# One encoder layer on TensorE: the weight tiles of the up-projection start 64 (or 112) bytes further on, and the down-projection's activations are loaded straight into their own tiles

## The chip, the cores and the metric

The kernel runs on one core of one Trainium2 chip. The metric is the time of one execution on the device in microseconds: 2622.09 us, the median of 3 runs (2621.0 to 2622.91).

## What is computed

One layer of a transformer trunk over 512 tokens of width 2048, all in float32: an input projection that feeds two attention branches and their gates, an output projection, and then a gated convolutional feed-forward part, which is the part that the change touches.

```python
h2 = rmsnorm(x, norm_ffn[l])
u = h2 @ w_up[l]                       # 2048 -> 2 * 5632
up = jnp.pad(u, ((0, 0), (1, 1), (0, 0)))
u = up[:, :-2] * cw[0] + up[:, 1:-1] * cw[1] + up[:, 2:] * cw[2] + conv_b[l]
gate, val = jnp.split(u, 2, axis=-1)
x = x + (jax.nn.silu(gate) * val) @ w_down[l]   # 5632 -> 2048
```

## The kernel before

**Number format.** Every float32 matrix product is made of three TensorE products of float32r numbers. A tensor is split into `hi`, its rounding to float32r, and `lo`, the rest (`split`, L222 to L233, for activations; `Plain.prep`, L146 to L160, for weights). ScalarE (ACT) makes `hi` with a copy, VectorE (DVE) makes `lo` with a subtraction. The products are hi by hi, hi by lo and lo by hi. All matmuls of the big products are issued by the helper `mm`, so they all stand under line L77 in the profile, and all loads on the queue of SyncE (SP) stand under L74, the helper `dma`, which keeps them in program order.

**Up.** `up(s)` for s from 0 to 21 makes one block of 256 gate and 256 value columns. Its product runs in `products`: 8 units, one for each pair of 128-row slices of the 2048 inputs. A unit has 7 forms of its weights (a scheme with seven products in place of eight), in two groups of 4 and 3. For each form and each half of the columns there are three matmuls, 42 in a unit and 7392 in all 22 blocks. In each of them the weights `wh` or `wl` (128 by 128) are the stationary operand, loaded by a LDWEIGHTS of its own, and 256 columns of a form of the activations, held in a slot `s`, stream past. `Product.load` brings a unit's weights into a tile `f` (4 buffers), and `Product.prep` (L581 to L595) splits them into the tiles `wh` and `wl`. In the built program the 56 slots, `wh` and `wl` all start at multiples of 512 bytes in a partition; the constants FILL and EDGE at the top of the kernel are pads that see to that.

After a block, `combine` copies the seven accumulators out of their PSUM banks (ACT L669, L671, L672 and DVE L666, L677), and the queue of small work does the rest: scaling by the row factor (DVE L828), the convolution (`conv`: six ACT instructions, L836, L838, L839, and then two accumulating DMAs on GpSimd's (POOL's) queue, L840 and L841), SiLU (ACT L853), the product of gate and value (DVE L857) and the store to the DRAM tensor `act[s]` (POOL L858).

**Down.** The 22 pairs of `act` are the activations of the down-projection, in two parts of 11. `down(part, n)` makes 512 output rows with 22 slices of the inner dimension, two in a unit of 24 matmuls; its matmuls stream 512 columns. Before a part runs, `split_act` loads each pair of `act` from DRAM and splits it: for part 0 in the last up block (one pair ahead of each unit from unit 1 on) and in the first four units of down, for part 1 in `down(0, 3)`. The load goes into a buffer `quad("a")`, 128 by 2 by 512, and ACT L227 and DVE L228 split it into four slots. There are two buffers of the tag "a", and they are the same ones into which `conv` writes its two shifted products `before` and `after`; they become free again when the accumulating DMAs L840 and L841 have read them.

Each engine runs its instructions in the order of the built program. On SP a load that waits for a buffer holds up all later loads; on ACT a split that waits for its load holds up all later ACT work.

Of the kernel before, what the change touches and what calls it, by code (L numbers as in the profile page):

```python
# [11 lines left out]
F32 = mybir.dt.float32  # L12
F32R = mybir.dt.float32r
AF = mybir.ActivationFunctionType
ALU = mybir.AluOpType
# [3 lines left out]
P = 128  # L19
# [19 lines left out]
def trunk_kernel(  # L39
# [6 lines left out]
    nc = tc.nc  # L46
# [17 lines left out]
    def slot(dt=F32):  # L64
        return big.tile([P, S], dt, tag="s", name="s", bufs=N_SLOTS)
# [4 lines left out]
    def bank(tag):  # L70
        return banks[tag].tile([P, S], F32, tag=tag, name=tag)

    def dma(dst, src):
        tc.keep_in_program_order(nc.sync.dma_start(dst, src))  # L74

    def mm(o, l, r, start, stop):
        nc.tensor.matmul(o, l, r, start=start, stop=stop, skip_group_check=True)  # L77
# [18 lines left out]
    part = {}  # L96
    for held, names in ((smalls, KEPT), (masks, SMALLS)):
        at = 0
# [16 lines left out]
    steps, units, queue = [], [], deque()  # L115
    at = {"load": 0, "sums": 0, "prep": 0, "use": 0}
# [10 lines left out]
    class Plain:  # L127


        def __init__(self, w, k, kpb, cols):  # L130
            self.w, self.k, self.kpb, self.cols = w, k, kpb, cols
# [14 lines left out]
        def prep(self, *between, pieces=1):  # L146
            self.load(pieces)
            for work in between:
                work()
            hi = wst["p"].tile([P, 1024], F32R, tag="hi", name="hi", bufs=2)  # L150
            lo = wst["p"].tile([P, 1024], F32R, tag="lo", name="lo", bufs=2)
            n = 1024 // pieces
            for c in range(0, 1024, n):
                nc.scalar.copy(hi[:, c:c + n], self.raw[:, c:c + n])  # L154
                nc.vector.tensor_tensor(  # L155
                    lo[:, c:c + n], self.raw[:, c:c + n], hi[:, c:c + n].bitcast(F32),
                    ALU.subtract)
            self.hi = hi.rearrange("p (a n) -> p a n", a=self.kpb)
            self.lo = lo.rearrange("p (a n) -> p a n", a=self.kpb)
# [12 lines left out]
    def advance(*between):  # L172


        prep_to(at["use"] + 1, between)
        for phase, d in (("sums", 2), ("load", 4)):
            while at[phase] < len(products_) and products_[at[phase]].ready(phase, at["use"] + d):
                getattr(products_[at[phase]], phase)()
                at[phase] += 1
        make_early()  # L180

    def next_unit():
        u = units[at["use"]]
        at["use"] += 1
        return u
# [38 lines left out]
    def split(src, alloc=slot, g=None):  # L224
        hi, lo = alloc(F32R), alloc(F32R)
        if g is None:
            nc.scalar.copy(hi, src)  # L227
            nc.vector.tensor_tensor(lo, src, hi.bitcast(F32), ALU.subtract)  # L228
        else:
            last["act"] = nc.scalar.activation(hi, src, AF.Copy, scale=g).ins  # L230
            last["dve"] = nc.vector.scalar_tensor_tensor(
                lo, src, g, hi.bitcast(F32), op0=ALU.mult, op1=ALU.subtract).ins
        return hi, lo  # L233
# [133 lines left out]
    def v_b(pair):  # L367
        raws, res = [], [None] * 2

        def evac(m, ps):  # L370
            v = att.tile([P, S], F32, tag="v", name="v", bufs=4)
            nc.scalar.copy(
                v.rearrange("p (j r c) -> p j r c", j=4, r=8),
                ps.rearrange("p (r j c) -> p j r c", j=4, r=8))
            raws.append(v)

        def head(h):
            v = raws[h].rearrange("p (j r c) -> p j r c", j=4, r=8)
            nc.vector.tensor_tensor(
                v, v, rows["m"].rearrange("p (r j c) -> p j r c", j=4, r=8), ALU.mult)  # L380
            b = bank("tr")
            for j in range(4):
                nc.tensor.transpose(
                    b[:, j * P:(j + 1) * P], raws[h][:, j * P:(j + 1) * P], ident)
            res[h] = split(b)

        step("f", w_in, [(C_VB + pair * 256, 256)], hT, evac,
             post=lambda: queue.extend(partial(head, h) for h in range(2)),
             rate=ATTENTION_RATE)
        return res  # L390
# [143 lines left out]
    v = v_b(0)  # L534
    q_a(1, ka, va)
    for pair in range(4):
        kq_b(pair, v)
        if pair < 3:
            v = v_b(pair + 1)
# [4 lines left out]
    ffn, products_, early, made = {}, [], deque(), deque()  # L544
    keep = tc.keep_in_program_order

    class Product:
# [1 line left out]

        def __init__(self, w, first, kept):
            self.w, self.first = w, first
            self.kept = dram.tile([P, 4, 256], F32, name=f"sums{first}") if kept else None
            self.made = False

# [25 lines left out]
        def prep(self, *between):  # L582
            self.parts = []
            for b, (tag, n) in enumerate((("a", 4), ("b", 3))):
                if between:
                    between[b]()
                hi = ffn["w"].tile([P, n, 256], F32R, tag="h" + tag, name="wh", bufs=2)
                lo = ffn["w"].tile([P, n, 256], F32R, tag="l" + tag, name="wl", bufs=2)
                f = self.f[:, 4 * b:4 * b + n]
                keep(nc.scalar.copy(hi, f))  # L590
                keep(nc.vector.tensor_tensor(lo, f, hi.bitcast(F32), ALU.subtract))  # L591
                self.parts += [(hi[:, i], lo[:, i]) for i in range(n)]
            for work in between[2:]:
                work()
# [16 lines left out]
    def quad(tag):  # L611
        return ffn["q"].tile([P, 2, S], F32, tag=tag, name=tag, bufs=2)
# [18 lines left out]
    def products(w, c, acts, evac, before=None, kept=()):  # L631

        def run():
            ps = []
            for i in range(8):
                if before:
                    before(i)
                u = next_unit()
                for f, (wh, wl) in enumerate(u.parts):
                    if i == 0:  # L640
                        ps.append(bank("mm"))
                    a = acts[i][f]
                    for m in range(2):
                        o, s = ps[f][:, m * 256:(m + 1) * 256], slice(m * P, (m + 1) * P)
                        mm(o, wh[:, s], a[:, :256], i == m == 0, False)
                        mm(o, wh[:, s], a[:, 256:], False, False)
                        mm(o, wl[:, s], a[:, :256], False, i == 7 and m == 1)
                advance(*(combine(ps, evac) if i == 7 else ()))
                run_queued(1)

        steps.append(run)
        v = w.rearrange("(d b p) (h n) -> d p b h n", b=2, p=P, h=2)
        for i in range(8):
            u = Product(v[i, :, :, :, c:c + 256], len(units), i in kept)
            units.append(u)
            products_.append(u)
            if i in kept:
                early.append(u)

    def combine(ps, evac):  # L660

        q1, q2, q4, q5, q7, q6, q3 = [p.rearrange("p (m n) -> p m n", m=2) for p in ps]
        v = lambda: scratch().rearrange("p (m n) -> p m n", m=2)
        top, low, p1, v2 = quad("u"), quad("u"), v(), v()
        left, right = slice(0, 256), slice(256, 512)
        add = lambda *args: keep(nc.vector.tensor_tensor(*args))  # L666

        def one():
            keep(nc.scalar.copy(p1, q1))  # L669
            add(top[:, :, left], q2, p1, ALU.add)  # L670
            keep(nc.scalar.copy(low[:, :, left], q4))  # L671
            keep(nc.scalar.copy(low[:, :, right], q5))  # L672

        def two():
            add(v2, p1, q6, ALU.subtract)
            add(p1, v2, low[:, :, right], ALU.add)
            keep(nc.vector.scalar_tensor_tensor(  # L677
                v2, q7, -1.0, v2, op0=ALU.mult, op1=ALU.subtract))
            add(top[:, :, right], q3, p1, ALU.add)

        def three():
            both = low.rearrange("p m (t n) -> p m t n", t=2)
            add(both, v2.unsqueeze(2).to_broadcast([P, 2, 2, 256]), both, ALU.subtract)
            evac(top, low)

        return one, two, three
# [24 lines left out]
    half = {}  # L711
# [113 lines left out]
    act = [dram.tile([P, 2, S], F32, name=f"act{j}") for j in range(pairs_ff)]  # L825
# [18 lines left out]
    parts = [range(pairs_ff // 2), range(pairs_ff // 2, pairs_ff)]  # L844
    acts = [[], []]
# [33 lines left out]

    def split_act(part, n):  # L880

        if n < len(parts[part]):
            a = quad("a")
            dma(a, act[parts[part][n]])
            acts[part] += [split(a[:, i]) for i in range(2)]

    def down(part, n):
        held = []
# [98 lines left out]
```

## Time and profile before

| | |
|---|---|
| median of 3 runs | 2622.09 us |
| the profiled execution | 2616.16 us |
| its span, first to last instruction | 2614.4 us |
| share of the span that TensorE is busy (PE) | 98% |
| mean granted TensorE clock | 0.993 |
| up, from its first to its last matmul | 1198.6 to 2111.4 us |
| down, from there to the last matmul | 2111.5 to 2610.4 us |

The busy share of PE is high everywhere and says little, because matmuls overlap: a matmul of 256 columns is shown 283 ns long, while the next one starts 120 ns after it. What counts is the distance between starts and the idle time between matmuls. In the groups, the tile names stand as output<-inputs, the streamed operand first: `mm<-s,wh` is a matmul of up, `mm<-s,hi` one of the other products. In the timeline, a row's two first numbers are its start and its length, xN merges N equal instructions, and the bracket gives the engine's idle time before it and what ended that.

### The profile page before, as it was taken

To read this page: it belongs to the slowest core of one execution; us is meant where nothing else is said; L and a number is where in the kernel's file an instruction comes from. 1 tells how busy PE (TensorE), PEld (TensorE's weight loads), DVE (VectorE), ACT (ScalarE), POOL (GpSimd) and SP (SyncE) were. 2 spreads that over 40 slices of the span, in tenths; PEclk is the share of its full clock that TensorE was granted. 3 is DMA by queue.
4 is the path that set the end of the run, shared out by engine and by line. 5 is a ranking of instruction groups with operands and counts; after the bars stand their busy time and mean duration, and the time that the engine had idled before them with its cause. 6 is when DMAs were issued, how large, how long until landed. Compare 5 with 4: busy or idle time off the path is not lost.

```text
span 2614.4 us, 38157 instructions
## 1 busy us (share of the span) xinstructions
PE 2568.2 (98%) x15016; PEld 2287.3 (87%) x15016; DVE 1521.3 (58%) x2155; ACT 1125.1 (43%) x1617; POOL 206.4 (8%) x248
## 2 busy tenths in 40 slices
PE   9999999999999999999999999999999879999999
PEld 7888888888888888888999999999999868888887
DVE  6565554635455567656778778787787543243222
ACT  5355544532222232334555665656656442132111
POOL 0100000000000000100111111111111100000000
PEclk9999999999999999999999999999999989999999
DMA  5322223338777888854677777777777755464443
GB/s 182 97 89 85 90 91 96 91 97 273 246 258 248 260 271 275 293 179 137 172 186 205 194 206 196 193 207 196 203 195 196 213 162 167 145 210 137 129 129 112
DMA packets 291509, 464.66 MB, mean 178 GB/s; under 512 B 22784, under 2 KB 190336, under 8 KB 291328
## 3 DMA queue, kind: packets, MB, share of 16 engines
q1 hardware_dynamic: 246240, 348.00, 42.4%
q0 software_dynamic: 40480, 105.83, 16.4%
q10 hardware_dynamic: 4608, 8.39, 0.8%
q8 instruction: 117, 1.92, 0.3%
q14 instruction: 64, 0.52, 0.1%
HBM read 347.93 MB, written 68.16 MB: 159 GB/s over the span
## 4 chain that ended last, share of the span: by engine, by line
PE 44%; DMA 3%; ACT 2%; issue 1%; DVE 0%; SPq 0%; ACTq 0%; POOLq 0%; DVEq 0%
PE mm L77 44%; DMA o<-a 2%; ACT wh L590 1%; ACT o L836 0%; DMA a<-act 0%; ACT a L838 0%; ACT a L839 0%; DMA f<-sums 0%; DMA raw<-in_w_down 0%; DMA f<-in_w_up 0%; DVE wl L591 0%; ACT t L669 0%; SPq L74 0%; ACT s L227 0%; ACT hi L154 0%
## 5 line engine op out<-in xcount | busy, mean ns | idle before, releaser
L77 PE MATMUL mm<-s,hi 128*128 128x512 f32 x3712 | 1111.1, 391 | 17.8 <-ACT t L669 8.4
L77 PE MATMUL mm<-s,wh 128*128 128x256 f32 x4928 | 848.2, 284 | 18.4 <-ACT wh L590 12.0
L77 PEld LDWEIGHTS mm<-s,hi 128*128 128x128 f32 x3712 | 699.2, 189 | 163.7 <-ACT t L669 8.9
L77 PEld LDWEIGHTS mm<-s,wh 128*128 128x128 f32 x4928 | 730.8, 193 | 20.3 <-ACT wh L590 12.8
L155 DVE TENSOR_TENSOR lo<-raw,hi 128x1024 fp32r<-128x1024 f32 (+1 forms) x289 | 352.6, 1220 | 661.6 <-ACT hi L154 649.6
L77 PE MATMUL mm<-s,lo 128*128 128x512 f32 x1856 | 683.1, 391 | 0.0
L154 ACT CAST hi<-raw 128x1024 fp32r<-128x1024 f32 (+1 forms) x289 | 303.4, 1050 | 848.6 <-PE mm L77 782.1
L77 PE MATMUL mm<-s,wl 128*128 128x256 f32 x2464 | 600.9, 284 | 0.8 <-DVE wl L591 0.8
L591 DVE TENSOR_TENSOR wl<-f,wh 128x1024 fp32r<-128x1024 f32 x352 | 375.1, 1088 | 157.5 <-ACT wh L590 152.5
L590 ACT CAST wh<-f 128x1024 fp32r<-128x1024 f32 x352 | 317.1, 939 | 300.9 <-PE mm L77 190.6
L77 PEld LDWEIGHTS mm<-s,wl 128*128 128x128 f32 x2464 | 432.0, 193 | 1.0 <-DVE wl L591 1.0
L77 PEld LDWEIGHTS mm<-s,lo 128*128 128x128 f32 x1856 | 349.5, 188 | 71.9
L77 PE MATMUL mm<-hi,s 128*128 128x512 f32 x896 | 285.5, 395 | 5.4 <-ACT hi L154 5.4
L77 PEld LDWEIGHTS mm<-hi,s 128*128 128x128 f32 x896 | 168.2, 189 | 38.3 <-ACT hi L154 5.4
L77 PE MATMUL mm<-lo,s 128*128 128x512 f32 x448 | 176.7, 396 | 0.0
L572 DVE TENSOR_TENSOR f<-f 128x512 f32<-128x512 f32 x176 | 120.5, 685 | 0.0
L77 PEld LDWEIGHTS mm<-lo,s 128*128 128x128 f32 x448 | 84.8, 189 | 16.8
L579 POOL DMA_DIRECT2D sums<-f x76 | 40.6, 535 | 574.3 <-DVE f L576 455.9
L840 POOL DMA_DIRECT2D o<-a x44 | 52.3, 1189 | 407.8 <-ACT a L838 391.4
L576 DVE TENSOR_TENSOR f<-f 128x256 f32<-128x256 f32 x176 | 74.7, 424 | 5.5
L575 DVE TENSOR_TENSOR f<-f 128x256 f32<-128x256 f32 x176 | 74.6, 424 | 5.3
L836 ACT ACTIVATE o<-u,smalls 128x512 f32<-128x512 f32 x88 | 71.1, 808 | 3.1 <-DVE o L857 1.5
(131 smaller groups left out, 1463.8 us busy)
## 6 DMA issues: line engine op xcount, KB each, us to landing
f<-in_w_up SPq DMA_DIRECT2D x252, 256.0 KB, 3.4
f<-in_w_up SPq DMA_DIRECT2D x428, 128.0 KB, 3.5
raw<-in_w_in SPq DMA_DIRECT2D x103, 512.0 KB, 3.9
raw<-in_w_down SPq DMA_DIRECT2D x88, 512.0 KB, 4.2
o<-a POOLq DMA_DIRECT2D x88, 511.0 KB, 5.4
sums<-f POOLq DMA_DIRECT2D x76, 512.0 KB, 5.3
f<-sums SPq DMA_DIRECT2D x76, 512.0 KB, 4.9
raw<-in_w_in SPq DMA_DIRECT2D x66, 256.0 KB, 3.0
```

The source lines that it names most:

```text
L77: nc.tensor.matmul(o, l, r, start=start, stop=stop, skip_group_check=True)
L154: nc.scalar.copy(hi[:, c:c + n], self.raw[:, c:c + n])
L155: nc.vector.tensor_tensor(lo[:, c:c + n], self.raw[:, c:c + n], hi[:, c:c + n].bitcast(F32), ALU.subtract)
L572: keep(nc.vector.tensor_tensor(f[:, 3:5], f[:, 2::-2], f[:, 6].unsqueeze(1).to_broadcast([P, 2, 256]), ALU.add))
L575: keep(nc.vector.tensor_tensor(f[:, 5], f[:, 4], f[:, 2], ALU.add))
L576: keep(nc.vector.tensor_tensor(f[:, 6], f[:, 5], f[:, 1], ALU.add))
L579: nc.gpsimd.dma_start(self.kept, self.f[:, 3:])
L590: keep(nc.scalar.copy(hi, f))
L591: keep(nc.vector.tensor_tensor(lo, f, hi.bitcast(F32), ALU.subtract))
L836: keep(nc.scalar.activation(o[:, m], u[:, m], AF.Identity, bias=cb[:, i:i + 1], scale=cw[:, i, 1:2]))
L840: nc.gpsimd.dma_start(o[:, :, 1:], before[:, :, :S - 1], accum_op=ALU.add)
```

## The change

There are two edits. The tiles of the split up weights grow by 32 floats (128 bytes), and the weights start inside them at float 16, which is 64 bytes beyond a multiple of 128, or for the first of the 8 units of a block at float 28, which is 112 bytes beyond. The streamed slots stay at multiples of 128. And `split_act` no longer uses `quad("a")`: each half of a pair is loaded into the slot that will hold its `lo`, `hi` is made from it into the other slot, and `lo` is then made in place.

```diff
-        def __init__(self, w, first, kept):
-            self.w, self.first = w, first
+        def __init__(self, w, first, kept, turn):
+            self.w, self.first, self.turn = w, first, turn
...
-                hi = ffn["w"].tile([P, n, 256], F32R, tag="h" + tag, name="wh", bufs=2)
-                lo = ffn["w"].tile([P, n, 256], F32R, tag="l" + tag, name="wl", bufs=2)
+                at = 28 if self.turn else 16
+                hi, lo = (
+                    ffn["w"].tile([P, n * 256 + 32], F32R, tag=half + tag, name="w" + half, bufs=2)[
+                        :, at:at + n * 256].rearrange("p (f n) -> p f n", f=n)
+                    for half in "hl")
...
-            u = Product(v[i, :, :, :, c:c + 256], len(units), i in kept)
+            u = Product(v[i, :, :, :, c:c + 256], len(units), i in kept, i == 0)
...
     def split_act(part, n):
-        if n < len(parts[part]):
-            a = quad("a")
-            dma(a, act[parts[part][n]])
-            acts[part] += [split(a[:, i]) for i in range(2)]
+        for i in range(2 * (n < len(parts[part]))):
+            hi, lo = slot(F32R), slot(F32R)
+            raw = lo.bitcast(F32)
+            dma(raw, act[parts[part][n]][:, i])
+            nc.scalar.copy(hi, raw)
+            nc.vector.tensor_tensor(lo, raw, hi.bitcast(F32), ALU.subtract)
+            acts[part].append((hi, lo))
```

In the built program the second edit shows on SP's queue in the last up block. The names are the tile that is loaded and the DRAM tensor that it comes from: `act2` to `act6` are pairs of down's activations, `f` and `raw` weights of up and of down. Before, SP has:

```order
L74 DMA f_20521<-sums375_234 128x1024
L74 DMA a_20536<-act2_139 128x1024
L74 DMA a_20596<-act3_140 128x1024
L74 DMA a_20657<-act4_141 128x1024
L74 DMA a_20718<-act5_142 128x1024
L74 DMA raw_20774<-in_w_down 128x2x512
L74 DMA a_20791<-act6_143 128x1024
L74 DMA raw_20847<-in_w_down 128x2x512
```

and now:

```order
L74 DMA f_20521<-sums375_234 128x1024
L74 DMA s_20537<-act2_139 128x512
L74 DMA s_20542<-act2_139 128x512
L74 DMA s_20597<-act3_140 128x512
L74 DMA s_20602<-act3_140 128x512
L74 DMA s_20658<-act4_141 128x512
L74 DMA s_20663<-act4_141 128x512
L74 DMA s_20719<-act5_142 128x512
L74 DMA s_20724<-act5_142 128x512
L74 DMA raw_20774<-in_w_down 128x2x512
L74 DMA s_20792<-act6_143 128x512
L74 DMA s_20797<-act6_143 128x512
```

Each load has become two of half the size, at the same place in the queue, and its target is a slot `s` in place of a buffer `a`. On ACT, at the end of the same block, before the change (a 128x512 CAST makes a `hi` of act6; `mm` is a PSUM bank, `u_20844` what `combine` makes; L836 to L839 are the convolution):

```order
L838 ACTIVATE a_20781<-u_20309,smalls_101 128x512
L839 ACTIVATE a_20782<-u_20309,smalls_101 128x512
L227 CAST s_20793<-a_20791 128x512
L227 CAST s_20797<-a_20791 128x512
L669 COPY t_20845<-mm_20333 128x512
```

and now:

```order
L842 ACTIVATE a_20781<-u_20309,smalls_101 128x512
L843 ACTIVATE a_20782<-u_20309,smalls_101 128x512
L890 CAST s_20791<-s_20792 128x512
L890 CAST s_20796<-s_20797 128x512
L673 COPY t_20845<-mm_20333 128x512
```

The order is the same; only the source of the two casts has changed. The matmuls are the same in number and form everywhere; in the last up block and the first units of down the scheduler has put some in another order (a unit begins with 14 matmuls of `wh`, where matmuls of `wl` stood between them).

## Prediction

> **What bounds the kernel now.** I read the page first, then the stages in windows, then the distance between matmul starts in the timeline, and last the waits of PE, ACT and SP where PE stands still.
>
> ```profile
> PE 2568.2 (98%) x15016; PEld 2287.3 (87%) x15016; DVE 1521.3 (58%) x2155; ACT 1125.1 (43%) x1617; POOL 206.4 (8%) x248
> L77 PE MATMUL mm<-s,wh 128*128 128x256 f32 x4928 | 848.2, 284 | 18.4 <-ACT wh L590 12.0
> L77 PE MATMUL mm<-s,wl 128*128 128x256 f32 x2464 | 600.9, 284 | 0.8 <-DVE wl L591 0.8
> ```
>
> PE is busy nearly always, and every matmul has a weight load of its own (x15016 on PE and on PEld). Up has 4928 + 2464 = 7392 matmuls of 256 columns. The next rows are stages: length, busy time and count on PE, PEld, DVE, ACT and POOL, granted clock, DMA share.
>
> ```profile
> 1205.00:2050.00 845.00, 841.70 (x7009) 840.89 (x7008) 652.52 (x828) 499.25 (x652) 106.15 (x98) 1.00 0.74 196
> ```
>
> Nearly all of up runs at 845 / 7009 = 0.1206 us a matmul, with DVE busy 77%, ACT 59% and DMA 74%: PE sets the pace. What sets PE's? First two rows of the timeline at the end of up:
>
> ```profile
> 2111.11 0.40 PE L77 MATMUL mm<-s,wh 128*128 128x256 f32 x2
> 2111.35 0.28 PE L77 MATMUL mm<-s,wl 128*128 128x256 f32 x1
> ```
>
> Two matmuls take 2111.35 - 2111.11 = 0.24 us, 120 ns each. Now the same after a pause, while the clock is granted at half: the window, and the first and the last of five rows of two matmuls.
>
> ```profile
> 2094.00:2099.00 5.00, 5.00 (x25) 0.50 0.56 210
> 2096.90 0.63 PE L77 MATMUL mm<-s,wh 128*128 128x256 f32 x2
> ...
> 2098.61 0.63 PE L77 MATMUL mm<-s,wh 128*128 128x256 f32 x2
> ```
>
> Four rows of two, 8 matmuls, go from 2096.90 to 2098.61 us, 213.8 ns each. At full clock the columns alone would take half of that, 106.9 ns; some 13 ns come on top, and they vanish at half clock. The window over down, with 512 columns a matmul:
>
> ```profile
> 2170.00:2611.00 441.00, 440.61 (x1944) 1.00 0.46 146
> ```
>
> That is 441 / 1944 = 226.9 ns, against 213.8 for twice 106.9: the same 13. So 13 ns go once per matmul, whatever its columns, and once per matmul there is one weight load beside it. That they collide at full speed is my reading, not a row. Two more places bear on it: a run of transposes (their group, with a mean length of 272 ns, and six in one row), and 512-column matmuls just after two transposes.
>
> ```profile
> L476 PE MATMUL tr<-ident,p 128*128 128x128 f32 x160 | 25.9, 272 | 0.0
> 506.45 0.82 PE L476 MATMUL tr<-ident,p 128*128 128x128 f32 x6
> 501.77 0.63 PE L77 MATMUL mm<-s,hi 128*128 128x512 f32 x2
> 502.24 0.39 PE L77 MATMUL mm<-s,lo 128*128 128x512 f32 x1
> 502.46 0.63 PE L77 MATMUL mm<-s,hi 128*128 128x512 f32 x2
> 502.93 0.39 PE L77 MATMUL mm<-s,lo 128*128 128x512 f32 x1
> ```
>
> The six transposes, which stream `ident` (it starts at byte 16608, not at a multiple of 128 like the rest), stand (0.82 - 0.272) / 5 = 109.6 ns apart. The five matmuls need (502.93 - 501.77) / 5 = 232 ns each, 5 more than in the steady state of down, with operands at the same places. The extra is thus no constant: it depends on how the two streams meet, and that is what a shift of addresses can touch.
>
> **Where PE stands still.** Three long pauses lie at the passage from up to down:
>
> ```profile
> 2093.53 1.01 PE L77 MATMUL mm<-s,wh 128*128 128x256 f32 x3 [8.05 <-ACT wh L590]
> 2121.46 0.80 PE L77 MATMUL mm<-s,hi 128*128 128x512 f32 x1 [8.44 <-ACT t L669]
> 2156.65 1.65 PE L77 MATMUL mm<-s,hi 128*128 128x512 f32 x3 [6.43 <-ACT hi L154]
> ```
>
> PE waits for ACT each time; ACT waits for a load of `act`, and SP, which should issue it, waits for the convolution's accumulating DMA. From 2072 to 2160 us:
>
> ```profile
> ACT s L227 <- DMA a<-act: 38.5, 10, 8.2
> SPq L74 <- DMA o<-a: 51.1, 5, 18.4
> ```
>
> Of the five waits of SP for `o<-a`, these are the three places, on POOL, on SP and, for the first, on ACT:
>
> ```profile
> 2083.37 1.18 POOL L840 DMA_DIRECT2D o<-a  x1 [4.12 <-ACT a L838]
> 2111.28 1.20 POOL L840 DMA_DIRECT2D o<-a  x1 [21.39 <-ACT a L838]
> 2143.76 1.18 POOL L840 DMA_DIRECT2D o<-a  x1 [5.70 <-ACT a L838]
> 2078.19 0.42 SPq L74 DMA_DIRECT2D f<-sums  x1
> 2088.21 11.56 SPq L74 DMA_DIRECT2D a<-act  x4
> 2116.21 0.32 SPq L74 DMA_DIRECT2D a<-act  x1
> 2148.70 0.32 SPq L74 DMA_DIRECT2D a<-act  x1
> 2082.98 0.71 ACT L839 ACTIVATE a<-u,smalls 128x512 f32<-128x512 f32 x1
> 2091.39 1.14 ACT L227 CAST s<-a 128x512 fp32r<-128x512 f32 x2 [7.71 <-DMA a<-act]
> ```
>
> A pair of POOL's issues begins at 2083.37, 2111.28 and 2143.76 us; some 5 us later SP goes on with `a<-act`, at 2088.21, 2116.21 and 2148.70; and ACT splits 3 us after that, at 2091.39.
>
> **The loads into the slots.** They take the buffers "a" out of this chain. What the three pauses cost, the cold clock after them included, comes from three windows:
>
> ```profile
> 2084.00:2111.40 27.40, 19.35 (x139) 0.81 0.49 134
> 2111.40:2149.00 37.60, 29.16 (x118) 0.86 0.58 168
> 2149.00:2170.00 21.00, 14.57 (x55) 0.84 0.70 200
> ```
>
> 27.40 - 139 x 0.120 = 10.7 us, 37.60 - 118 x 0.227 = 10.8, 21.00 - 55 x 0.227 = 8.5: together 30. What is late next: SP has nothing to issue after 2078.61 us but act2, so its halves go out nearly 10 us earlier. ACT is busy until 2083.69 (2082.98 + 0.71), splits two halves (1.14) and rounds the weights, while PE needs these at 2085.2, so about 1 us of the first pause stays. In the second the split of act6 still stands between the convolution and the copy that frees a PSUM bank: again about 1 us. I take 28.
>
> The new wait is for the slots: a load now waits until PE has read its slot for the last time, and behind it on SP stand the loads of weights. By the order of the built program the slots of act0 to act10 are last read between a tenth of unit 0 and unit 6.4 of the last block, each before the load comes up; in `down(0, 3)` act14 needs a slot that PE reads within the first unit, three units before that split. Nothing should wait. Two half loads cost one issue more on SP, some 0.3 us as in the rows above. How long loads of both sizes take to land:
>
> ```profile
> a<-act SPq DMA_DIRECT2D x22, 512.0 KB, 5.1
> t<-out_a SPq DMA_DIRECT2D x8, 256.0 KB, 3.2
> s<-in_x_t SPq DMA_DIRECT2D x32, 256.0 KB, 5.8
> ```
>
> Loads of 256 KB land after 3.2 to 5.8 us, the 512 KB one after 5.1: no dearer. ACT and DVE do the same splits, and starting `wl` later in the last block's units can only relieve a wait. If one of the pauses stays after all, the gain is 18 to 20; if all vanish, 30.
>
> **The shifted weights.** No row of before shows an up matmul with its weights elsewhere, so I bound it. The nearest row below is the transposes' 109.6 ns: 7392 x 10.4 ns = 77 us gained. Above, the disturbed rows' 5 ns more: 7392 x 5 = 37 us lost. In between I take half of the extra, 120 to 113.3 ns, 7392 x 6.7 = 49 us: the shift is half of 128 bytes, so I expect the streams to meet less, and have no row that says they never meet. This is a choice. The other 112 bytes concern an eighth of the matmuls and I give them no price of their own. ACT and DVE write `wh` and `wl` at the new place in the same form: nothing, hidden under DVE's 23% of free time.
>
> The Trainium skill speaks against this term: TensorE: Matmul & The Clock Gate, in "Step-by-step: what each phase is for", gives matmul and weight load two independent read ports and says "Loading the next tile's weights doesn't steal SBUF read bandwidth from the running matmul"; by that rule addresses change nothing. The trace does not fit the spacing that the same page gives in "Back-to-back issue gap", columns / 2.4 + 2.5 ns, which is 109.2 ns for 256 columns, where up shows 120.
>
> What is given back: a block's 336 matmuls get 2.2 us shorter, and ACT, DVE and DMA must follow; 59%, 77% and 74% become at most 63%, 82% and 79%. PE's waits at block ends, for the copies of the accumulators, between 1205 and 2050 us:
>
> ```profile
> PE mm L77 <- ACT t L669: 3.3, 4, 1.5
> ```
>
> That is 3.3 us in four waits. If each of the four grew by 2.2 it would be 9 us; I take 4.
>
> **Sum.** 2616.2 (the profiled execution) - 28 - 49 + 4 = 2543. The median of the runs is 5.9 us above the profiled execution, which gives 2549 us.
>
> **The rivals.**
> First, the 13 ns are a fixed price of a matmul at full clock, and only the loads help: 2622 - 28 = 2594. For it speaks that 256 and 512 columns pay the same; against it the transposes' 109.6 and the disturbed 232. The quoted sentence of the skill's page says the same as this rival.
> Second, the streams no longer meet at all: spacing as of the transposes, 2622 - 28 - 77 + 6 = 2523, 6 being given back at the block ends. Against it: these transposes may differ in more than an address.
> Third, the slower side: up falls into the disturbed pattern, 5 ns more a matmul: 2622 - 28 + 37 = 2631. It decides from 33 / 7392 = 4.5 ns on, because the loads' 28 us and another 5 have to be lost first. For it: the present steady state is the better one of the two that the 512-column rows show.
> Fourth, the change does nothing that counts: the extra is fixed and the loads, now held by slots, pause SP as long as the buffers did: 2622.
>
> **How the numbers follow.** About half of the extra goes (111 to 118 ns, 2526 to 2585 us): 0.47. Loads alone: 0.25. All of it: 0.12. Slower: 0.10. Nothing: 0.06. About 0.2% (5 us) is what a measurement of this kernel can tell from no change. Faster: 0.47 + 0.25 + 0.12 = 0.84; same 0.06; slower 0.10. The range reaches from below the second rival to above the first, 2515 to 2602 us, and leaves out the third and the fourth and some tails, 0.2 together.
>
> **What would show it.** Right: starts in up some 113 ns apart at full clock while down keeps 227; no `a<-act` and no wait of SP for `o<-a` around 2080 us; PE idle for at most 1 or 2 us at each of the three places. The second edit is wrong if PE still waits over 4 us for ACT there; the first if up's starts stay 120 ns apart or go beyond 124.

## The result and the profile after

The changed kernel takes 2582.41 us (median of 4 runs, 2578.96 to 2588.31) against 2621.55 us for the kernel before beside it (4 runs): a ratio of 0.9857, 95% interval 0.9834 to 0.9881, 39 us less. The profiled execution is the slowest of the four, 2588.31 us with a span of 2586.5, so its sums come out some 6 us above the median. In the kernel after, lines stand 4 to 8 further on: the copies after a block are L673 to L676 (L669 to L672 before), silu L857 (L853), the conv's accumulating DMAs L844 and L845 (L840, L841), the splits of `act` L890 and L891 (L227, L228).

The page's engine row and the two groups of up, after (busy us, mean ns of one | idle before, releaser):

```profile
PE 2537.2 (98%) x15016; PEld 2254.9 (87%) x15016; DVE 1517.3 (59%) x2155; ACT 1123.6 (43%) x1617; POOL 206.4 (8%) x248
L77 PE MATMUL mm<-s,wh 128*128 128x256 f32 x4928 | 826.3, 281 | 33.6 <-ACT t L673 24.3
L77 PE MATMUL mm<-s,wl 128*128 128x256 f32 x2464 | 589.9, 280 | 2.3 <-DVE wl L595 2.3
```

The busy time of up's two groups has fallen from 1449 to 1416 us, but the idle time in front of `wh` has risen from 18.4 to 33.6, and its releaser has changed, from the cast of `wh` to the copy L673 at the end of a block. So something was gained inside the blocks and part of it lost between them. Both can be seen apart. In one block of up the windows run from the start of unit 1 to that of unit 3, and from there to the end of unit 7 (PE alone). Before:

```profile
1654.31:1664.39 10.08, 10.08 (x87) 1.00 0.65 158
1664.39:1689.59 25.20, 25.20 (x213) 1.00 0.84 233
```

and after:

```profile
1649.49:1659.34 9.85, 9.85 (x86) 1.00 0.66 161
1659.34:1683.14 23.80, 23.80 (x212) 1.00 0.83 228
2170.00:2580.00 410.00, 410.00 (x1811) 1.00 0.45 142
```

The windows were cut at the starts of units, so they hold 2 x 42 = 84 and 5 x 42 = 210 starts (the counts take in those that lie across an edge). Before, a start comes every 25.20 / 210 = 120.0 ns and 10.08 / 84 = 120.0; after, every 23.80 / 210 = 113.3 ns in units 3 to 7, but 9.85 / 84 = 117.3 in units 1 and 2. The last row is down: 410 / 1811 = 226.4 ns, as before. Over all blocks, the mean by unit from 0 to 7 is 119.0, 117.7, 117.1, 113.9, 113.3, 113.6, 113.6, 113.5 ns, together 115.15. Unit 0 is the one at 112 bytes; it gains almost nothing, and the two units after it, which are at 64 bytes, take time to come down.

The end of a block: waits between 1205 and 2050 us (total, times, longest). Before, PE's wait for the copies stood at 3.3 us in 4 waits, and ACT's wait at silu at:

```profile
ACT o L853 <- DMA o<-a: 36.5, 18, 4.3
```

After:

```profile
PE mm L77 <- ACT t L673: 21.2, 16, 3.1
ACT o L857 <- DMA o<-a: 70.1, 19, 7.3
```

What lies behind one of the 16 is in the timeline, after, at the start of the block above, which began at 1642.65 us: first PE, then ACT.

```profile
1643.24 0.28 PE L77 MATMUL mm<-s,wl 128*128 128x256 f32 x1
1645.10 0.51 PE L77 MATMUL mm<-s,wh 128*128 128x256 f32 x2 [1.57 <-ACT t L673]
...
1637.97 1.06 ACT L857 ACTIVATE o<-o 128x1024 f32<-128x1024 f32 x1 [3.86 <-DMA o<-a]
1638.94 1.77 ACT L594 CAST wh<-f 128x1024 fp32r<-128x1024 f32 x2
1640.61 0.81 ACT L840 ACTIVATE o<-u,smalls 128x512 f32<-128x512 f32 x1
...
1643.87 0.70 ACT L843 ACTIVATE a<-u,smalls 128x512 f32<-128x512 f32 x1
1644.48 0.56 ACT L673 COPY t<-mm 128x512 f32<-128x512 f32 x1
```

PE stops at 1643.24 + 0.28 us, a few matmuls into the new block, since it needs the bank that the copy at 1644.48 empties. ACT comes late: it stood 3.86 us at silu (L857) for the second accumulating DMA, and had the casts and six conv instructions (from 1640.61) to do before the copy. In the kernel before, where the same block began at 1649.27 us, the same two rows are:

```profile
1642.25 1.06 ACT L853 ACTIVATE o<-o 128x1024 f32<-128x1024 f32 x1 [2.10 <-DMA o<-a]
1648.97 0.56 ACT L669 COPY t<-mm 128x512 f32<-128x512 f32 x1
```

There the copy started just before the block did, and PE did not wait for it.

The passage from up to down in the same three windows, after (PE's busy time is the second number):

```profile
2084.00:2111.40 27.40, 24.05 (x160) 22.37 (x161) 20.93 (x28) 21.86 (x33) 2.40 (x2) 0.94 0.94 270
2111.40:2149.00 37.60, 37.60 (x167) 31.13 (x167) 16.44 (x17) 18.35 (x25) 5.36 (x5) 1.00 0.59 159
2149.00:2170.00 21.00, 21.00 (x95) 17.38 (x94) 7.76 (x9) 4.15 (x4) 2.88 (x4) 1.00 0.88 251
```

What is left of the pauses there, and what ends the first, in the timelines of PE, SP and ACT:

```profile
2086.49 2.48 PE L77 MATMUL mm<-s,wh 128*128 128x256 f32 x14 [3.94 <-ACT wh L594]
2104.98 0.74 PE L77 MATMUL mm<-s,hi 128*128 128x512 f32 x2 [0.86 <-ACT t L673]
...
2076.16 6.18 SPq L74 DMA_DIRECT2D s<-act  x8
2084.24 1.25 ACT L890 CAST s<-s 128x512 fp32r<-128x512 f32 x2 [3.54 <-DMA s<-act]
```

PE is busy throughout the last two windows: the third pause is gone. Of the first 3.94 us are left (the first window begins inside it), of the second 0.86, now at 2104.98. SP goes on at 2076.16 us instead of 2088.21, but now eight half loads go out in a row, the DMA share of the window is 0.94 (0.49 before), and ACT waits 3.54 us for the halves of act2. In the same stretch SP's waits hold no `o<-a` (51.1 us before), and the wait for the slots is small:

```profile
SPq L74 <- PE mm L77: 1.6, 5, 0.5
```

The books between the two profiled spans, 2614.4 and 2586.5: matmul distance -7392 x 4.84 ns = -35.8; pauses in down -19.1; in up, the pause at 2086 us included, time lost between matmuls (waits and slow clock after them) 24.5 to 52.2, +27.7. The sum is -27.2, the spans differ by -27.9. Of the lost time 18.5 us before and 12.2 after lie in the last block, the first pause above all; in the 21 blocks ahead of it 6.1 us became 40.0. So in this execution waits in these blocks took back 33.9 us, nearly all that the shorter distance had gained in these blocks.

### The profile page after: what moved, and what is told of

It is laid out like the page before. It is cut to its first block, busy times and chain, and to the rows that moved or that the text cites. A ratio compares the mean times of both kernels' runs of the same rounds, so it can differ in the third digit from the quotient of the medians.

```text
span 2586.5 us, 38229 instructions
## 1 busy us (share of the span) xinstructions
PE 2537.2 (98%) x15016; PEld 2254.9 (87%) x15016; DVE 1517.3 (59%) x2155; ACT 1123.6 (43%) x1617; POOL 206.4 (8%) x248
## 4 chain that ended last, share of the span: by engine, by line
PE 88%; ACT 5%; DMA 4%; issue 2%; DVE 1%; SPq 0%; POOL 0%; ACTq 0%; POOLq 0%; DVEq 0%
PE mm L77 85%; DMA o<-a 3%; PE tr L77 2%; ACT wh L594 1%; ACT o L840 1%; ACT a L843 1%; ACT a L842 1%; PE tr L476 1%; PE tr L334 0%; DMA f<-in_w_up 0%; DVE wl L595 0%; ACT t L673 0%; DMA f<-sums 0%; DMA s<-act 0%; SPq L74 0%
## 5 line engine op out<-in xcount | busy, mean ns | idle before, releaser
L77 PE MATMUL mm<-s,wh 128*128 128x256 f32 x4928 | 826.3, 281 | 33.6 <-ACT t L673 24.3
L77 PEld LDWEIGHTS mm<-s,wh 128*128 128x128 f32 x4928 | 712.6, 190 | 38.5 <-ACT t L673 27.8
L77 PE MATMUL mm<-s,wl 128*128 128x256 f32 x2464 | 589.9, 280 | 2.3 <-DVE wl L595 2.3
L77 PEld LDWEIGHTS mm<-s,wl 128*128 128x128 f32 x2464 | 424.1, 190 | 2.9 <-DVE wl L595 2.9
L844 POOL DMA_DIRECT2D o<-a x44 | 52.3, 1189 | 380.7 <-ACT a L842 364.8
L840 ACT ACTIVATE o<-u,smalls 128x512 f32<-128x512 f32 x88 | 71.1, 808 | 3.1 <-DVE o L861 0.8
```

The costliest lines, as they stand in the source:

```text
L840: keep(nc.scalar.activation(o[:, m], u[:, m], AF.Identity, bias=cb[:, i:i + 1], scale=cw[:, i, 1:2]))
L844: nc.gpsimd.dma_start(o[:, :, 1:], before[:, :, :S - 1], accum_op=ALU.add)
```

## The experiments

The table puts all runs together. "Distance" is where up's weights start beyond the slots' residue, modulo 128 bytes; "ns" is the mean distance between the starts of neighbouring up matmuls in the trace, those over 140 ns left out; "lost" is what these longer distances hold beyond 115 ns, in us, in the one profiled execution. A time with "1 run" is one execution. Each ratio is to runs of the kernel before taken beside it, whose medians lie between 2617.94 and 2621.55 us.

| kernel | distance | us | ratio to before | ns | lost |
|---|---|---|---|---|---|
| before | 0 | 2621.55 | | 120.0 | 24.5 |
| after | 64, unit 0: 112 | 2582.41 | 0.9857 [0.9834, 0.9881] | 115.2 | 52.2 |
| loads only | 0 | 2594.19 | 0.9909 [0.9892, 0.9925] | 120.0 | 21.1 |
| shift only | 64, unit 0: 112 | 2602.27 | 0.9933 [0.9917, 0.9948] | 115.1 | 46.3 |
| all 64 | 64 | 2575.96 | 0.9841 [0.9822, 0.9861] | 113.7 | 44.7 |
| 128 bytes | 0 | 2591.25, 1 run | | 119.2 | 19.6 |
| all 32 | 32 | 2588.71, 1 run | | 119.0 | 17.6 |
| all 80 | 80 | 2585.71, 1 run | | 117.7 | 30.7 |
| all 96 | 96 | 2590.93, 1 run | | 117.2 | 29.2 |
| all 112 | 112 | 2601.92, 1 run | | 119.8 | 24.0 |
| slots moved along | 0 | 2595.09, 1 run | | 119.1 | 17.9 |
| all 64, small work earlier | 64 | 2577.72 | 0.9837 [0.9824, 0.9850] | 113.9 | 45.7 |
| all 64, gate conv earlier | 64 | 2544.46 | 0.9725 [0.9712, 0.9738] | 114.0 | 12.5 |
| before, gate conv earlier | 0 | 2607.87 | 0.9957 [0.9941, 0.9974] | 120.0 | 18.3 |

### The two edits apart

Loads alone: the up weights go back to where they were.

```diff
-                at = 28 if self.turn else 16
-                hi, lo = (
-                    ffn["w"].tile([P, n * 256 + 32], F32R, tag=half + tag, name="w" + half, bufs=2)[
-                        :, at:at + n * 256].rearrange("p (f n) -> p f n", f=n)
-                    for half in "hl")
+                hi = ffn["w"].tile([P, n, 256], F32R, tag="h" + tag, name="wh", bufs=2)
+                lo = ffn["w"].tile([P, n, 256], F32R, tag="l" + tag, name="wl", bufs=2)
```

> Only the second edit: down's activations are loaded straight into their slots, the up weights stay at multiples of 512 bytes. If the two edits act apart, as I hold: starts in up stay 120 ns apart, the pauses at the passage to down go as in the changed kernel (about 19 us in down and 6 in the last up block), and waits at the block ends of up stay at some 3 us, so 2594 to 2600 us. If the whole gain came from the shifted weights: 2622 us.

2594.19 us beside 2618.31 (before, in the same comparison): -24.1.

The shift alone: `split_act` as before.

```diff
-        for i in range(2 * (n < len(parts[part]))):
-            hi, lo = slot(F32R), slot(F32R)
...
+        if n < len(parts[part]):
+            a = quad("a")
+            dma(a, act[parts[part][n]])
+            acts[part] += [split(a[:, i]) for i in range(2)]
```

> Only the first edit: the shifted weights, with the old loads through the buffers. Spacing theory: up's starts come down to about 115 ns, 36 us less, PE gives some 25 us of that back in waits for ACT at the block ends, and the three pauses at the passage to down stay, so 2608 to 2616 us. If the new waits at the block ends came from the other edit: about 2586 us. If the shift does nothing by itself: 2622 us.

2602.27 us: -16.0. The two add up to -40.1, and the change measured -39.1, so within the spread of the runs they act apart. The time lies 6 us under the range I had expected. The shift's matmuls are 7392 x 4.86 ns = 35.9 us shorter, but 21.8 us more were lost between them (24.5 to 46.3), by the same row as in the kernel after:

```profile
PE mm L77 <- ACT t L673: 20.1, 12, 3.1
```

### Which distance, and what the first unit does

```diff
-                at = 28 if self.turn else 16
+                at = 16
```

> As the changed kernel, but every unit's weights lie 64 bytes on, the first unit's too. If the other place in the first unit is what moves the streams into the 113 ns pattern: up's starts stay near 118 ns in all units, matmul time in up is 21 us longer, some 10 to 15 us of it hidden by shorter waits at the block ends, so about 2590 us. If the first unit at 112 is only a slower place (119 ns): units 0 to 2 come down towards 113, and the time is 2575 to 2582 us.

2575.96 us, ratio 0.9841; as its interval overlaps with that of the change, the times alone do not separate the two. The distances do: 113.7 ns for 115.2, and units 0 to 2 at 114.6, 114.1 and 113.3 where the change has 119.0, 117.7 and 117.1. So 7392 x 1.44 = 10.6 us of the change's matmul time go to the 112 bytes of an eighth of the units.

Then other distances, each for all units. First a whole 128 bytes, which leaves the residue as it was:

```diff
-                at = 28 if self.turn else 16
+                at = 32
```

> As the changed kernel, with the same larger tiles, but all up weights start 128 bytes into them. If only the distance modulo 128 bytes between weights and streamed operand counts: starts 120 ns apart again, time as with the loads alone, 2594 to 2600 us. If it is the pad, or being off a multiple of 512 bytes: about 115 ns and 2582 us.

119.2 ns, one run of 2591.25 us: the distance modulo 128 decides nearly all, the move of the tiles itself 0.8 ns. The other values of `at` are 8 (32 bytes), 28 (112), 24 (96) and 20 (80):

> As the changed kernel, all up weights 32 bytes beyond the streamed slots' residue. If a spacing of 113 ns needs the two streams in opposite halves of 128 bytes: starts in up 116 to 119 ns apart, about 2590 us. If any distance of at least 32 bytes does: about 113.5 ns, about 2576 us. If 32 meets worse than 0: over 120 ns, over 2597 us.

> As the changed kernel, all up weights 112 bytes on, as it has them in the first unit of a block alone. If the place sets the spacing: 117 to 119 ns in all units, as in the changed kernel's first units, so about 2590 us. If it only sets off a slow passage into another pattern: units behind the first come down to 113 ns, about 2578 us.

> All up weights 96 bytes beyond the activations' residue. If the spacing is a narrow dip at 64 (32 gave 119.0, 64 gave 113.7, 112 gave 119.75): 119 to 120 ns, 2590 to 2600 us. If it is a slope on the upper side that 112 only ends: 116 to 118 ns, 2580 to 2590 us. 113.7 ns and 2576 us would say that any multiple of 32 from 64 on serves.

> All up weights 80 bytes beyond. If only a whole 64 helps: 119 to 120 ns, 2590 to 2600 us. If the distance counts by degrees between 64 and 112: about 115 to 117 ns, 2578 to 2588 us. As at 64: 113.7 ns, 2576 us.

They gave 119.0, 119.8, 117.2 and 117.7 ns. By these runs 64 is the best of the places tried; 80 and 96 keep part of the gain, and it is all but gone at 32 and at 112 (where I had expected 117 to 119). The distance modulo 128 is not all: with 80 bytes the units 3, 5 and 7 stand at 116.7 ns and 2, 4 and 6 at 118.4 to 118.8, and the two kinds of unit use different ones of the two buffers of the weight tiles. No run takes that apart. The 96-byte run takes longer than the 80-byte one though its starts lie closer together; by the traces that time lies outside up's matmuls: up begins 3.3 us later, and the pauses at the start of down come to 4.4 us for 0.7.

Is it the distance between the two streams, or the place of the weights? The pad FILL moves the slots and up's weights by 64 bytes together; down's weights stay where they were, so that down gets the distance of 64.

```diff
-FILL, EDGE = 124, 120
+FILL, EDGE = 140, 120
...
-                at = 28 if self.turn else 16
+                at = 0
```

> The loads as in the changed kernel; the pad ahead of the slots is 64 bytes longer, so the slots and the up weights both start 64 bytes beyond a multiple of 128, while down's weights, on the other side of the memory, stay at multiples of 128. If only the distance between the two operands counts: up stays at 120 ns, and down, where the distance is now 64, falls below 226.7, to about 220 ns if it gains as up did (1.3 to 1.4 times 1000 of 2112 matmuls by 6.7 ns, 14 us in all), so about 2582 us. If the address itself counts: up about 113 to 115 and down 226.7.

Up has 119.1 ns although its weights lie at 64, so the distance counts and not the place. Down went against what I expected (some 220 ns). Its window in this run:

```profile
2170.00:2580.00 410.00, 410.00 (x1793) 1.00 0.46 145
```

That is 410 / 1793 = 228.7 ns for 226.4: the distance that saves 6 ns on up's 256 columns costs 2 on down's 512. It is one run, and it does not show whether the length of the matmul makes the difference or something else in which the two stages differ.

### Where the time at the block ends comes from

First the whole queue of small work one place (a unit) earlier, on top of all 64 (`wait` is an empty place):

```diff
-                wait, partial(scale, gate), pending_act.pop(),
+                partial(scale, gate), pending_act.pop(),
                 lambda: held.update(g=conv(gate, 2 * s)), wait, partial(scale, val), silu,
-                lambda: held.update(v=conv(val, 44 + 2 * s))))
+                lambda: held.update(v=conv(val, 44 + 2 * s)), wait))
```

> As the kernel with all weights at 64 bytes, and the small work behind a block (scaling, convolution, SiLU) starts one unit earlier in the next block, so that ACT's convolution of the values is done a unit before the copies of the accumulators. If the waits that grew at the block ends (about 22 us) come from ACT standing behind the convolution's accumulating DMAs: most of them go, 15 to 20 us less than with all weights at 64, 2556 to 2562 us. If they come from somewhere else, such as DMA or DVE being short: 2576 us, no change.

It brought nothing: 2577.72 us. PE's waits for the copy L673 are gone, but between 1205 and 2050 us the trace shows waits for DVE in their place, and ACT stands at silu even longer than with all 64 (67.3 us):

```profile
ACT o L857 <- DMA o<-a: 86.8, 19, 8.7
PE mm L77 <- DVE u L670: 15.8, 18, 0.9
```

Silu had moved with the conv that it waits for. So the next run moves the gate half's conv, with the scaling and the previous block's product that stand ahead of it, and leaves val's scaling, silu and val's conv in their places:

```diff
-                wait, partial(scale, gate), pending_act.pop(),
-                lambda: held.update(g=conv(gate, 2 * s)), wait, partial(scale, val), silu,
+                partial(scale, gate), pending_act.pop(),
+                lambda: held.update(g=conv(gate, 2 * s)), wait, wait, partial(scale, val), silu,
```

> All up weights at 64 bytes as in the run that gave 2576, and of each unit's small work only the gate half's conv is taken one place earlier, so that the two accumulating DMAs have a unit's time more before silu needs what they leave. Theory A (up's waits at the block ends come from ACT standing at silu for the second accumulating DMA, with val's conv and the weights' copies behind it): the `ACT t` row of TensorE's waits in up falls from 21.8 to under 8 us, up's waits from 33.6 to about 18, time 2558 to 2564. Theory B (the copies come late because of the amount of ACT's work between two units, wherever silu stands): waits 30 to 37, time 2573 to 2580. The earlier run that moved the whole small work one place earlier gave 2578 and speaks for B, but there conv of val moved with it.

2544.46 us, ratio 0.9725: 31 us less than all 64, more than I had expected. Its window over most of up, with PE at 837.97 of 845 us, and its waits in that window:

```profile
1205.00:2050.00 845.00, 837.97 (x7318) 836.77 (x7317) 680.62 (x860) 528.85 (x694) 111.49 (x103) 1.00 0.79 209
```

```profile
ACT o L857 <- DMA o<-a: 24.3, 19, 4.2
PE mm L77 <- ACT t L673: 2.4, 2, 1.9
```

All 64 has in these two rows:

```profile
ACT o L857 <- DMA o<-a: 67.3, 19, 7.9
PE mm L77 <- ACT t L673: 21.8, 16, 3.1
```

ACT's wait at silu falls from 67.3 us to 24.3, PE's wait for the copies from 21.8 to 2.4, the lost time in up from 44.7 to 12.5, which makes up the 31 us. The distance of starts stays at 114.0. From the previous run this order differs only in that val's scaling, silu and val's conv stand one place later, so it is the room between the gate's conv and silu that counts. This shows the chain: ACT's wait for the accumulating DMAs reached PE through the copies behind it. It is also the fastest version of the study.

How much of that was there before the change? The same order in the kernel before:

> The kernel before with conv of the gate half one place earlier, as in the run that gave 2544, and nothing of the change. Theory A (the waits at up's block ends were there before in small, 18 us with 6 us of slow clock behind them, and the change made them more by running each block sooner): about two thirds of these 24 us go, 2600 to 2608, and of the 31 us that this order gave with all weights at 64 bytes, some 15 us were new with the change. Theory B (they are as large here): 2586 to 2594. Theory C (at 120 ns per matmul the copies come early enough, and these waits have another cause): 2614 to 2622.

2607.87 us, ratio 0.9957: -10, where the change's kernel with all 64 gained 31. ACT's wait at silu falls there from 36.5 us to

```profile
ACT o L853 <- DMA o<-a: 2.6, 4, 1.3
```

So some 20 us of the waits were new: the shorter block had turned a wait on ACT that mostly hid into one that PE feels. At the block ends it was more still: in the first 21 blocks this order lowers the lost time from 6.1 to 3.9 us here, with all 64 from 32.7 to 6.6. Most of the 10 us come from the pauses around the passage to down.

## Why the prediction was right and where it was not

The direction, the two causes and the range held; the point lay 33 us too low, since two terms of the sum were mis-sized, both to the same side.

**What bounds the kernel.** Right in that the extra over the columns' own time depends on how the two streams' addresses stand to each other; that the weight load is what the stream collides with remains my reading. The Trainium skill, TensorE: Matmul & The Clock Gate, "Step-by-step: what each phase is for", has two independent read ports, by which the shift alone would have changed nothing. The shift alone gave 115.1 ns for 120.0 and 2602.27 us for 2618.31, and the measurement decides. By "Back-to-back issue gap" on the same page of the Trainium skill, the 109.2 ns that I held against the trace are the gap of an isolated matmul. So up's 120 ns did not test them. The first rival (2594) fell: that time came from the loads alone. And the 13 ns are not one price for both lengths: 64 bytes took some 6 ns from up and, in one run, added 2 to down.

**The loads, -28.** Alone they gave -24.1. The third pause went whole. Of the other two, about 1 us each was to stay. In the change 3.94 and 0.86 us stayed; with the loads alone it was the other way round:

```profile
2092.83 1.93 PE L77 MATMUL mm<-s,wh 128*128 128x256 f32 x14 [1.30 <-ACT wh L590]
2114.07 1.22 PE L77 MATMUL mm<-s,hi 128*128 128x512 f32 x2 [2.92 <-ACT t L669]
```

For the first I had taken the landing times of before, 3.2 to 5.8 us, but half loads issued between 2070 and 2090 us in the change took 8.4 us (median), eight of them in a row, at a DMA share of 0.94. With the loads alone they took 7.7 us (issued between 2080 and 2096 us) and the pause was 1.30, so the crowd can be only part of the cause; no run tries it by itself. The wait for slots cost next to nothing (1.6 us), as forecast.

**The shifted weights, -49.** Measured -35.8 in the profiled execution. The choice of 113.3 ns was near to what a distance of 64 gives when every unit has it (113.7, -46.4), but that was luck: the lower bound that it was set against, the transposes' 109.6 ns, is no spacing of such a matmul, since their rows show 128x128, half as many columns, and `ident` and `p` are plain float32. The step that failed is "The other 112 bytes concern an eighth of the matmuls and I give them no price of their own": that unit ran at 119.0 ns and the next two at 117.7 and 117.1, which is 10.6 us.

**Given back, +4.** Measured about +20: the shift alone gained 16.0 us where its matmuls were 35.9 us shorter. The step that failed is the one that let four waits grow by a block's 2.2 us, and took the engines' shares (63%, 82%, 79%) as a sign of room. The waits grew in number, from 4 to 12 in the shift alone and 16 in the change, as more blocks crossed the point where the copies come late. ACT had time enough; it spent it standing at silu. I had not read the row of before that showed this, 36.5 us of ACT's wait for `o<-a`.

**The sum.** -28 - 49 + 4 = -73 was forecast; -24 - 36 + 20 = -40 is what the runs show, and -39 was measured. With the first unit at 64 and the gate's conv a place earlier the kernel does reach 2544 us, but that takes two further edits, and the order alone gives 10 us without the change too.

## What to carry to other kernels

When the bound engine gets faster, look not only at the others' busy shares but at each in-order wait on them that ends shortly before the bound engine needs something: a wait that only just hid comes out once a stage gets shorter. Here a block's matmuls got 336 x 4.84 ns = 1.6 us shorter, and PE's 4 waits became 16. To take such a wait away, put distance between the producer and the waiting instruction; here moving both together only moved the wait. And where operands' addresses count, price every unit that differs, take bounds only from matmuls of the same shape and number format, and measure each shape by itself.

## What the runs showed of the hardware

- With 128 by 128 float32r weights loaded for every matmul and 256 columns streamed, at full clock, the distance between starts depends on the weights' place against the streamed operand modulo 128 bytes: 119.1 to 120.0 ns at 0, 119.0 at 32, 113.7 at 64, 117.7 at 80, 117.2 at 96, 119.8 at 112. Each place but 0 and 64 is one run.
- In down, with 512 columns, the 64 bytes cost: 228.7 ns for 226.4, in one run.
- Ten half loads of 256 KB that were issued within 20 us, eight of them in a row, took 8.4 us to land (median), where the median of all 44 is 5.0.
- A slower pattern outlasts its cause: units at 64 bytes that follow one at 112 ran at 117.7 and 117.1 ns before the mean came down to 113.3 to 113.9. Why it settles only after two units, no run tells.
